# A position-bias table for eight attention heads: replicated in DRAM and read skewed, or stored once and turned round by a matrix product

## The chip, the cores and the metric

The kernel runs on one core of one Trainium2 chip. The metric is the device time of one execution in microseconds (us), taken as the median over runs. TensorE does the matrix products (PE in the profile, with its weight loads as PEld), VectorE (DVE) and ScalarE (ACT) do elementwise work, GpSimd (POOL) does some elementwise work and issues some DMAs, and SyncE (SP) issues nearly all DMAs. One DMA is carried out by up to 16 DMA engines.

## The reference, cut to what matters

The program is one decoder layer over 256 tokens with 16 meta tokens in front (L = 272 positions): layer norm, a token mixer of two parallel branches, a second norm, and a mixture of 32 experts. The part that the change touches is the relative-position bias of the sparse attention branch. `rel_bias` has 32 buckets by 8 heads, and a bucket depends on the distance between query and key alone:

```python
bias = rel_bias[t5_bucket(q_pos[None, :, None] - sel)].astype(jnp.float32)
logits = logits + jnp.moveaxis(bias, -1, 2)
```

For one head the bias of query p and key c is thus a function of c - p: a 128-row table of which each row is the row above it shifted by one place. The kernel keeps these tables as one tile `Wb` of 128 partitions x 8 heads x 272 numbers, and one tile serves both blocks of 128 queries (the first block uses its last 144 columns).

## The kernel before, in words

**The whole.** All loads of weights go through SP, in 1 MB pieces, into three rotating buffers (`load_w`, line 111; pool `wp`, `bufs=3`). ScalarE makes the high part of each weight half-piece (line 121) and VectorE the low part (line 122), and TensorE multiplies both with the normalised input. `fgroup` (line 239) is one such projection of 256 columns: two pieces, each in two halves, and after each half a call of `step()`. `step` (line 230) advances the first two generators of the list `bg`, so that small background work is laid between the halves of the large products; `drain` runs all of them to their end. The order of projections is: qk0 to qk3, mv0 to mv3, iq0 and iq1, then for each pair of heads aq, ak, av, then mo, the merge gates, the output projection, and last the experts, whose weights (some 400 MB) stream in through the same SP queue.

**The bias table.** `t5_bias` (line 301) is put on `bg` after the first projection qk0. A matrix product of `relb` and the one-hot matrix `hot` gives one row of 400 numbers for each of 8 heads, VectorE copies it to `rsb` (8 partitions x 400, line 307), and GpSimd issues a DMA (line 309) that writes every head's row 128 times into the DRAM tile `rdr` (8 x 128 x 400 numbers, 1600 KB). `t5_load` (line 311) is called after iq0: four DMAs on SP (line 314) read `rdr` back, two heads each. Their access pattern starts at element 127 and goes 399 elements from one partition to the next, so that partition p gets its head's row from element 127 - p on:

```python
late(nc.gpsimd.dma_start(out=rdr, in_=rsb.unsqueeze(1).to_broadcast([8, P, 400])))
...
in_=bass.AP(rv.tensor, rv.offset + h * P * 400 + 127, [[399, P], [P * 400, 2], [1, L]])
```

The wrapper `late` keeps an instruction in the order of the program; other instructions may be moved by the framework's scheduler.

**Who uses it.** `attend` (line 561) adds `Wb[:, h]` and a mask on GpSimd (line 564), once for each of 8 heads and 2 query blocks. Its units are put on `bg` after the first av projection. Before them, `index_scores` (line 515) is on `bg`: it scores the keys in 16 small products (`pi`, line 527), two to a step, each followed by a ScalarE activation (line 530), and picks the top keys on VectorE. These products take their PSUM tiles from the pool `px`, which has three buffers (`pxt`, line 102).

Of the kernel before, what the change touches and what calls it, by code (L numbers as in the profile page):

```python
# [11 lines left out]
F32 = mybir.dt.float32  # L12
# [5 lines left out]
ALU = mybir.AluOpType  # L18
# [4 lines left out]
P = 128  # L23
# [4 lines left out]
L = S + NM  # L28
# [3 lines left out]
AH = 8  # L32
# [15 lines left out]
def trunk(ctx, tc, x, meta, ln_emb_g, ln_emb_b, rel_bias, w_in, conv_w, conv_b, b_ig, b_fg,  # L48
          mh_g, w_pm, w_pa, w_out, ln1_g, ln1_b, w_group, b_group, w_router, b_router,
          w_gu, w_dn, ln2_g, ln2_b, t5hot, out, dbg=None):  # L50
    nc = tc.nc
    x = x[0]
    out = out[0]
# [9 lines left out]
    dram = ctx.enter_context(tc.tile_pool(name="dram", bufs=1, space=DRAM))  # L63

    late = tc.keep_in_program_order
# [36 lines left out]
    def pxt(name):  # L102
        return px.tile([P, 512], F32, name=name, tag="x")

    def pzt(name):
        return pz.tile([P, 512], F32, name=name, tag="z")
# [37 lines left out]
    ap_ = at_ctx.enter_context(tc.tile_pool(name="ap", bufs=1, side="right"))  # L144
# [7 lines left out]
    for i in (1, 2):  # L152
        for c in range(4):
# [7 lines left out]
                           in_=conv_w[0].rearrange("t (c p) -> (t c) p", p=P)))  # L161
# [11 lines left out]
    Wb = ap_.tile([P, AH, L], F32, name="Wb")  # L173
# [54 lines left out]
    bg = []  # L228
# [6 lines left out]
    def drain():  # L235
        while bg:
            step(len(bg))

    def fgroup(c0, name, t0=0, raw0=None):

        n = L - t0
        nk = 8
        pts = [pmt(f"{name}_p{i}") for i in range(2)]
        for kc in range(KD // nk):
            raw = raw0 if raw0 and not kc else load_w(w_in, kc * nk, nk, c0, 256,
                                                      f"{name}_r{kc}")
            if raw0 and kc:
                small_loads()
            for hf in range(2):
                if raw0:  # L250
                    k = kc * nk + hf * 4
                    for k in range(k + 2 if k else 0, min(k + 6, KD)):
                        embed(k)
                wh, wl = split_w(raw[:, hf * 4:hf * 4 + 4], f"{name}_{kc}{hf}")
                k0 = kc * nk + hf * 4
                for kk in range(4):
                    k = k0 + kk
                    for i in range(2):
                        for r in (xhk, xlk):
                            nc.tensor.matmul(pts[i][:, :n], lhsT=wh[:, kk, i * P:i * P + P],  # L260
                                             rhs=r(k, slice(t0, L)), start=k == 0 and r is xhk,
                                             stop=False)
                for kk in range(4):
                    k = k0 + kk
                    for i in range(2):
                        nc.tensor.matmul(pts[i][:, :n], lhsT=wl[:, kk, i * P:i * P + P],
                                         rhs=xhk(k, slice(t0, L)), start=False, stop=k == KD - 1)
                step()
        return pts
# [26 lines left out]
        late(nc.vector.tensor_copy(col[:, 0:40], pcol[:, 0:40]))  # L296
        late(nc.vector.tensor_copy(col[:, 72:136], pcol[:, 40:104]))

    rdr = dram.tile([8, P, 400], F32, name="rdr")

    def t5_bias():


        pr = pzt("pr")
        nc.tensor.matmul(pr[:8, :400], lhsT=relb, rhs=hot, start=True, stop=True)
        rsb = mp_.tile([8, 400], F32, name="rsb")
        nc.vector.tensor_copy(rsb, pr[:8, :400])
        yield
        late(nc.gpsimd.dma_start(out=rdr, in_=rsb.unsqueeze(1).to_broadcast([8, P, 400])))

    def t5_load():
        rv = rdr[:]
        for h in range(0, AH, 2):
            late(nc.sync.dma_start(
                out=Wb[:, h:h + 2],
                in_=bass.AP(rv.tensor, rv.offset + h * P * 400 + 127,
                            [[399, P], [P * 400, 2], [1, L]])))


    qk = mp_.tile([P, 8, L], F32, name="qk")  # L320
# [194 lines left out]
    def index_scores():  # L515
        pw = pzt("pw")
        for b in range(2):
            nc.tensor.transpose(pw[:, b * 16:b * 16 + 12], iwf[64:76, b * P:b * P + P],
                                ident[64:76, 64:76])
        nc.vector.tensor_copy(iw, pw[:, :32].rearrange("p (a b) -> p a b", a=2)[:, :, 4:12])  # L520
        for b in range(2):
            nk = 144 + b * 128
            s = bp.tile([P, L], F32, name=f"sc{b}", tag="sc", bufs=2)
            for h in range(8):
                r0 = (h % 2) * 64
                pi = pxt(f"pi{b}{h}")
                nc.tensor.matmul(pi[:, :nk], lhsT=iq[r0:r0 + 64, h // 2, b * P:b * P + P],
                                 rhs=ik[r0:r0 + 64, :nk], start=True, stop=True)
                rl = bp.tile([P, L], F32, name=f"rl{b}{h}", tag="rl", bufs=2)
                nc.scalar.activation(rl[:, :nk], pi[:, :nk], AF.Relu)  # L530
                if h == 0:
                    nc.vector.tensor_scalar(s[:, :nk], rl[:, :nk], iw[:, b, h:h + 1], None,
                                            op0=ALU.mult)
                else:
                    nc.vector.scalar_tensor_tensor(s[:, :nk], rl[:, :nk], iw[:, b, h:h + 1],
                                                   s[:, :nk], op0=ALU.mult, op1=ALU.add)
                if h % 2:
                    yield
            nc.gpsimd.memset(s[:, 0:NM], BIG)
            nc.gpsimd.affine_select(s[:, :nk], s[:, :nk], pattern=[[-1, nk]],  # L540
                                    compare_op=ALU.is_ge, fill=-BIG, base=16 + b * 128,
                                    channel_multiplier=1)
            w = bp.tile([P, L], F32, name=f"wk{b}", tag="wk", bufs=2)
            m8 = bp.tile([P, 8], F32, name=f"m8{b}", tag="m8", bufs=2)
            cur = s
            for r in range(TOPK // 8):
                nc.vector.max(m8, cur[:, :nk])
                nc.vector.match_replace(w[:, :nk], m8, cur[:, :nk], LOW)
                cur = w
            nc.vector.max(m8, w[:, :nk])  # L550
            nc.vector.memset(m8[:, TOPK % 8:], LOW)
            nc.vector.match_replace(w[:, :nk], m8, w[:, :nk], LOW)
            mk = msk[b]
            nc.vector.tensor_scalar(w[:, :nk], w[:, :nk], -2e38, -BIG, op0=ALU.is_gt,
                                    op1=ALU.mult)
            nc.vector.tensor_scalar(mk[:, :nk], s[:, :nk], -0.5 * BIG, -BIG, op0=ALU.is_le,
                                    op1=ALU.mult)
            nc.vector.tensor_tensor(mk[:, :nk], mk[:, :nk], w[:, :nk], op=ALU.min)
# [41 lines left out]
    def tokens_then(fts, name, v, units):  # L600
        to_tokens(fts, name, False, v)
        yield
        for g in units:
            bg.append(g)

    bg.append(index_scores())
    for j in range(AH // 2):
        pq = fgroup(O_AQ + j * 256, f"aq{j}", t0=16)
        aq = bp.tile([P, 2, S], F32, name=f"aq{j}", tag="aq", bufs=2)
        for i in range(2):  # L610
            nc.scalar.mul(aq[:, i], pq[i][:, :S], SC)
        pk = fgroup(O_AK + j * 256, f"ak{j}")
        ak = bp.tile([P, 2, L], F32, name=f"ak{j}", tag="ak", bufs=2)
        for i in range(2):
            nc.scalar.copy(ak[:, i], pk[i][:, :L])
        pv = fgroup(O_AV + j * 256, f"av{j}")
        drain()
        v = []
        units = [attend(2 * j + i, b, aq[:, i], ak[:, i], v, i * P)
                 for i in range(2) for b in range(2)]  # L620
        bg.append(tokens_then(copy_out(pv, f"av{j}"), f"av{j}", v, units))
# [574 lines left out]
    for pr_ in range(NE // 2):  # L1196
# [39 lines left out]
        if pr_ < LAST:  # L1236
            pys = [pyp.tile([P, 512], F32, name=f"py{pr_}_{c}", tag="py") for c in range(4)]
            for kk in range(4):
                ws = [next_w(), next_w()]
                for c in range(4):  # L1240
                    for i in range(2):
                        nc.tensor.matmul(pys[c][i * 64:i * 64 + 64], lhsT=hTs[i][:, kk],  # L1242
                                         rhs=ws[i][:, 0, c * 512:c * 512 + 512], start=kk == 0,
                                         stop=kk == 3)
                issue()
            pend += [lambda c=c, py=py, f=gated: f(c * 512, 512, py) for c, py in enumerate(pys)]
        else:
            flush()
            for c0, n in LASTP:
                ws = [next_w(), next_w()]  # L1250
                py = pyp.tile([P, 512], F32, name=f"py{pr_}_{c0}", tag="py")
                for kk in range(4):
                    for i in range(2):
                        nc.tensor.matmul(py[i * 64:i * 64 + 64, :n], lhsT=hTs[i][:, kk],
                                         rhs=ws[i][:, kk], start=kk == 0, stop=kk == 3)
# [17 lines left out]
    with tc.If(nmax > C):  # L1273
        with tc.For_i(0, NE, 1) as e:
# [4 lines left out]
            for part in range(2):  # L1279
                base = C + part * P  # L1280
# [13 lines left out]
                for k in range(KD):  # L1294
                    pd = op.tile([P, 512], F32, name=f"opd{k}" + nn, tag="o1")
                    for i, part in enumerate((uh, ul)):
                        for b in range(2):
                            nc.tensor.matmul(pd[:, :P], lhsT=part[:, b, rows_of(k)],
                                             rhs=oh[:, b], start=i == 0 and b == 0,
                                             stop=i == 1 and b == 1)  # L1300
# [3 lines left out]
                for kc in range(8):  # L1304
# [3 lines left out]
                    for kk in range(2):  # L1308
                        k = kc * 2 + kk
                        for i in range(2):  # L1310
                            nc.tensor.matmul(pgs[i], lhsT=xo[:, k],
                                             rhs=w[:, kk, i * 512:i * 512 + 512],
                                             start=k == 0, stop=k == KD - 1)
# [6 lines left out]
                for c in range(4):  # L1320
# [4 lines left out]
                    for kk in range(4):  # L1325
                        nc.tensor.matmul(py, lhsT=hT[:, kk], rhs=w[:, kk], start=kk == 0,
                                         stop=kk == 3)
                    nc.scalar.copy(ysb, py)
                    for b in range(2):
                        pc = op.tile([P, 512], F32, name=f"opc{c}{b}" + nn, tag="og1")  # L1330
                        nc.tensor.matmul(pc, lhsT=cwo[:, b * P:b * P + P], rhs=ysb, start=True,
                                         stop=True)
# [70 lines left out]
```

## Time and profile before

| | us |
|---|---|
| median of 3 runs | 1806.74 |
| lowest and highest of them | 1804.3, 1811.79 |
| the profiled execution | 1807.82 |
| its span, first to last instruction | 1806.1 |
| TensorE busy in the span | 1718.2 |
| VectorE, ScalarE, GpSimd busy | 711.8, 455.6, 111.0 |

The span is what the rows below are counted in: a time in a row is a distance from its start. The 1.7 us between span and execution time lie outside it. A busy share says how long an engine had an instruction in flight, not that it ran at its peak.

### The profile page before, as it was taken

What the parts mean: (1) busy time and instruction counts of PE and PEld (TensorE: products, weight loads), DVE (VectorE), ACT (ScalarE), POOL (GpSimd) and SP (SyncE); (2) the same over time, 40 slices, a digit from 0 to 9 for tenths busy, and PEclk for the clock granted to TensorE, in tenths of its full rate; (3) what the DMA queues carried; (4) which work ended last, traced back from release to release, by engine and by line L of the source; (5) the groups of instructions that cost most, each with busy time, mean ns of one, the idle gap of its engine ahead of it and who ended that gap; (6) DMA issues with size and microseconds to landing.
All of it is one profiled execution on the core that took longest, in us unless ns stands there. A gap on an engine that the chain in (4) does not pass through costs nothing. (4 is left out here: it accounts for less than half of the span.)

```text
span 1806.1 us, 21173 instructions
## 1 busy us (share of the span) xinstructions
PE 1718.2 (95%) x8626; PEld 1043.8 (58%) x8626; DVE 711.8 (39%) x1204; ACT 455.6 (25%) x703; POOL 111.0 (6%) x131
## 2 busy tenths in 40 slices
PE   8599999999999999999999999999999999999996
PEld 7598899988787877874343343333433434334332
DVE  7356774454556456552232242122112221222024
ACT  5243444444343444342010110110101101101010
POOL 3000210001122022000000000000000000000002
PEclk8799999999999999999999999999999999999998
DMA  7634454447565568458999999999999999999992
GB/s 219 129 117 142 141 164 140 148 156 247 173 213 173 198 217 295 171 212 343 419 403 408 413 356 421 421 391 421 421 420 420 422 420 421 420 422 420 421 402 71
DMA packets 155925, 538.67 MB, mean 298 GB/s; under 512 B 15772, under 2 KB 64116, under 8 KB 107680
## 3 DMA queue, kind: packets, MB, share of 16 engines
q1 hardware_dynamic: 153120, 530.54, 76.4%
q0 software_dynamic: 2640, 6.72, 1.9%
q8 instruction: 69, 1.13, 0.3%
q14 instruction: 32, 0.26, 0.0%
q10 hardware_dynamic: 64, 0.02, 0.0%
HBM read 533.50 MB, written 3.74 MB: 297 GB/s over the span
## 5 line engine op out<-in xcount | busy, mean ns | idle before, releaser
L1078 PE MATMUL gu<-we,xe 128*64 128x512 f32 x1016 | 455.9, 597 | 0.0
L1080 PE MATMUL gu<-we,xe 128*64 128x512 f32 x1016 | 454.5, 597 | 0.0
L1242 PE MATMUL py<-we,hT 128*64 128x512 f32 x960 | 276.8, 611 | 0.0
L1078 PEld LDWEIGHTS gu<-we,xe 128*64 128x64 f32 x1016 | 131.7, 137 | 244.2 <-issue 230.1
L1085 DVE TENSOR_TENSOR hb<-gu,hb 64x512 f32<-64x512 f32 x32 | 22.0, 689 | 349.1 <-ACT hb L1084 349.1
L1242 PEld LDWEIGHTS py<-we,hT 128*64 128x64 f32 x960 | 82.1, 137 | 123.8 <-issue 113.5
L1080 PEld LDWEIGHTS gu<-we,xe 128*64 128x64 f32 x1016 | 131.5, 137 | 17.2 <-issue 16.1
L1084 ACT ACTIVATE hb<-gu 64x512 f32<-64x512 f32 x32 | 18.9, 591 | 422.5 <-PE gu L1080 422.5
L1192 DVE TENSOR_TENSOR acc<-pc,acc 128x512 f32<-128x512 f32 (+1 forms) x122 | 77.5, 677 | 76.3 <-PE pc L1186 76.3
L1231 ACT ACTIVATE yh<-py,gsl 128x512 fp32r<-128x512 f32 (+1 forms) x65 | 42.7, 679 | 255.4 <-PE py L1242 178.7
L1232 DVE SCALAR_TENSOR_TENSOR yl<-py,gsl,yh 128x512 fp32r<-128x512 f32 (+1 forms) x65 | 46.7, 736 | 139.1 <-ACT yh L1231 138.7
L1009 DVE TENSOR_SCALAR xe<-pxe,gbp 128x256 f32<-128x256 f32 x64 | 34.8, 544 | 111.3 <-PE pxe L1002 111.3
L1002 PEld LDWEIGHTS pxe<-oh,uh 128*128 128x128 f32 x256 | 40.6, 197 | 48.3 <-DVE xe L1009 27.9
L1186 PE MATMUL pc<-yh,ohT 128*128 128x512 f32 (+1 forms) x130 | 53.9, 438 | 14.5 <-DVE acc L1192 11.6
L1006 ACT ACTIVATE xe<-pxe,gbp 128x256 f32<-128x256 f32 x64 | 36.0, 563 | 106.9 <-PE pxe L1002 106.9
L1002 PE MATMUL pxe<-oh,uh 128*128 128x256 f32 x256 | 59.6, 315 | 2.0 <-DMA acc<-in_w_gate_up_dram 2.0
L1178 POOL TENSOR_TENSOR fin<-acc,fin 128x512 f32<-128x512 f32 (+1 forms) x10 | 10.3, 1052 | 785.7 <-DVE acc L1192 785.7
L1186 PEld LDWEIGHTS pc<-yh,ohT 128*128 128x128 f32 x130 | 23.0, 188 | 55.6 <-issue 37.5
L1002 PE MATMUL pxe<-oh,ul 128*128 128x256 f32 x256 | 52.1, 285 | 0.0
L1186 PE MATMUL pc<-yl,ohT 128*128 128x512 f32 (+1 forms) x130 | 51.3, 418 | 0.8 <-DVE yl L1232 0.7
L1088 PEld LDWEIGHTS ph<-ident,hb 64*128 64x128 f32 x128 | 17.8, 210 | 44.3 <-DVE hb L1085 43.5
L1002 PEld LDWEIGHTS pxe<-oh,ul 128*128 128x128 f32 x256 | 41.1, 199 | 0.0
(920 smaller groups left out, 3109.7 us busy)
## 6 DMA issues: line engine op xcount, KB each, us to landing
we<-in_w_gate_up_dram SPq DMA_DIRECT2D x254, 1024.0 KB, 15.0
we<-in_w_down_dram SPq DMA_DIRECT2D x126, 1024.0 KB, 13.2
gm_r<-in_w_in_dram SPq DMA_DIRECT2D x16, 1024.0 KB, 5.0
ga_r<-in_w_in_dram SPq DMA_DIRECT2D x16, 1024.0 KB, 5.1
wo_r<-in_w_out_dram SPq DMA_DIRECT2D x16, 1024.0 KB, 5.1
qk_r<-in_w_in_dram SPq DMA_DIRECT2D x8, 1024.0 KB, 6.4
mv_r<-in_w_in_dram SPq DMA_DIRECT2D x8, 1024.0 KB, 5.3
aq_r<-in_w_in_dram SPq DMA_DIRECT2D x8, 1024.0 KB, 5.2
```

The costliest lines, as they stand in the source:

```text
L1002: nc.tensor.matmul(pt[:, :4 * C], lhsT=part[:, b, rows_of(k)], rhs=ohf[:, b], start=i == 0 and b == 0, stop=i == 1 and b == 1)
L1006: nc.scalar.activation(xe[:, k], pt[:, :4 * C], AF.Identity, bias=gbp[:, 1, k:k + 1], scale=gbp[:, 0, k:k + 1])
L1009: nc.vector.tensor_scalar(xe[:, k], pt[:, :4 * C], gbp[:, 0, k:k + 1], gbp[:, 1, k:k + 1], op0=ALU.mult, op1=ALU.add)
L1078: nc.tensor.matmul(pg_[other], lhsT=lt, rhs=w[:, kk, 0:512], start=k == 0, stop=k == KD - 1)
L1080: nc.tensor.matmul(pg_[mine], lhsT=lt, rhs=w[:, kk, 512:1024], start=k == 0, stop=k == KD - 1)
L1084: nc.scalar.activation(hb[mine], pg_[other], AF.Silu)
L1085: nc.vector.tensor_tensor(hb[mine], pg_[mine], hb[mine], op=ALU.mult)
L1186: nc.tensor.matmul(pc[:, :n], lhsT=ohT[:, b * P:b * P + P], rhs=y[:, :n], start=i == 0, stop=i == 1)
L1192: nc.vector.tensor_tensor(av, pc[:, :n], av, op=ALU.add)
L1231: nc.scalar.activation(yh[:, :n], py[:, :n], AF.Copy, scale=gate)
L1232: nc.vector.scalar_tensor_tensor(yl[:, :n], py[:, :n], gate, yh[:, :n].bitcast(F32), op0=ALU.mult, op1=ALU.subtract)
L1242: nc.tensor.matmul(pys[c][i * 64:i * 64 + 64], lhsT=hTs[i][:, kk], rhs=ws[i][:, 0, c * 512:c * 512 + 512], start=kk == 0, stop=kk == 3)
```

## The change

The row of each head is written to DRAM once (8 x 400 numbers). The read-back keeps four DMAs of two heads, 128 partitions and rows of 272, but partition p starts at element p of its head's row, so that the rows of the table arrive in reverse order. A new generator `t5_flip` makes an anti-diagonal one-hot matrix `anti` with two GpSimd instructions, then for each head multiplies `anti` with `Wb[:, h]` on TensorE, which puts the rows in the right order in PSUM, and copies the result back into `Wb[:, h]` on ScalarE. It is put on `bg` behind `index_scores`, and yields after `anti` and after each head.

```diff
-    rdr = dram.tile([8, P, 400], F32, name="rdr")
+    rdr = dram.tile([8, 400], F32, name="rdr")
...
-        late(nc.gpsimd.dma_start(out=rdr, in_=rsb.unsqueeze(1).to_broadcast([8, P, 400])))
+        late(nc.gpsimd.dma_start(out=rdr, in_=rsb))
...
-                in_=bass.AP(rv.tensor, rv.offset + h * P * 400 + 127,
-                            [[399, P], [P * 400, 2], [1, L]])))
+                in_=bass.AP(rv.tensor, rv.offset + h * 400, [[1, P], [400, 2], [1, L]])))
+
+    def t5_flip():
+        anti = ap_.tile([P, P], F32, name="anti")
+        nc.gpsimd.memset(anti, 0.0)
+        nc.gpsimd.affine_select(anti, anti, pattern=[[1, P]], compare_op=ALU.not_equal, fill=1.0,
+                                base=1 - P, channel_multiplier=1)
+        yield
+        for h in range(AH):
+            pw = pxt(f"pfl{h}")
+            nc.tensor.matmul(pw[:, :L], lhsT=anti, rhs=Wb[:, h], start=True, stop=True)
+            nc.scalar.copy(Wb[:, h], pw[:, :L])
+            yield
...
     bg.append(index_scores())
+    bg.append(t5_flip())
```

## Rows read from the trace of the kernel before

**Rows 1.** Stretches: length, busy us of PE, PEld, DVE, ACT, POOL, clock, DMA, GB/s.

```profile
60.00:70.00 10.00, 3.18 (x26) 2.97 (x24) 0.00 (x0) 0.00 (x0) 0.00 (x0) 0.79 0.50 56
70.00:80.00 10.00, 0.00 (x0) 0.00 (x0) 0.00 (x0) 0.00 (x0) 0.00 (x0) 0.50 0.53 83
80.00:90.00 10.00, 7.60 (x47) 7.61 (x48) 6.87 (x11) 3.90 (x5) 0.00 (x0) 0.69 0.80 264
...
210.00:220.00 10.00, 10.00 (x83) 9.32 (x80) 6.03 (x13) 4.75 (x11) 0.42 (x2) 1.00 0.41 121
...
1300.00:1400.00 100.00, 96.13 (x415) 35.58 (x412) 21.08 (x35) 9.69 (x17) 0.00 (x0) 1.00 1.01 420
```

**Rows 2.** Waits: engine, line, releaser: us in total, times, longest.

```profile
PE qk_p L260 <- ACT qk_00h L121: 19.2, 1, 19.2
...
ACT qk_00h L121 <- DMA qk_r<-in_w_in_dram: 23.7, 1, 23.7
...
SPq L808 <- PE wo_p L284: 22.1, 5, 10.8
```

**Rows 3.** DMA issues: count, KB each, median us from issue to landing.

```profile
aq_r<-in_w_in_dram SPq DMA_DIRECT2D x8, 1024.0 KB, 5.2
...
rdr<-rsb POOLq DMA_DIRECT2D x1, 1600.0 KB, 36.6
Wb<-rdr SPq DMA_DIRECT2D x4, 272.0 KB, 5.9
...
mhg<-in_mh_norm_g_dram POOLq DMA_DIRECT2D x1, 512.0 KB, 3.7
```

**Rows 4.** Line 309's issue (ns, start us); queue in 60:82 (packets, MB, engines' share).

```profile
L309 POOL DMA_DIRECT2D rdr<-rsb x1: 1117/1117/1117, 42.7 to 42.7; - x1
...
q0 software_dynamic: 194, 0.88, 39.9%
```

**Rows 5.** SP's issues in order of time: start us, us, what.

```profile
58.55 19.59 SPq L113 DMA_DIRECT2D mv_r<-in_w_in_dram  x1
...
148.50 2.28 SPq L314 DMA_DIRECT2D Wb<-rdr  x4
166.41 5.10 SPq L113 DMA_DIRECT2D iq_r<-in_w_in_dram  x2
```

**Rows 6.** PE in order of time around the gap: start us, us, [idle before].

```profile
62.02 1.17 PE L266 MATMUL qk_p<-xh,qk_11l 128*128 128x272 f32 x8
...
82.40 0.60 PE L260 MATMUL qk_p<-xh,qk_00h 128*128 128x272 f32 x1 [19.21 <-ACT qk_00h L121]
...
86.19 1.18 PE L266 MATMUL qk_p<-xh,qk_00l 128*128 128x272 f32 x8
87.20 0.29 PE L260 MATMUL qk_p<-xh,qk_01h 128*128 128x272 f32 x1
```

**Rows 7.** PE in order of time, later: plain f32 products, and a short gap.

```profile
187.20 0.70 PE L461 MATMUL pn<-mv3b,e 128*128 128x257 f32 x2
187.83 0.70 PE L461 MATMUL pn<-mv3m,e 16*128 16x257 f32 x2
...
202.05 1.22 PE L266 MATMUL iq_p<-xh,iq_11l 128*128 128x256 f32 x8 [1.14 <-DVE iq_11l L122]
...
253.72 0.86 PE L566 MATMUL pl<-ak,aq 128*128 128x144 f32 x4
254.22 0.48 PE L260 MATMUL aq_p<-xh,aq_11h 128*128 128x256 f32 x1
```

**Rows 8.** ACT and POOL in order of time; line 402 (min/median/max ns).

```profile
182.98 1.05 ACT L121 CAST iq_00h<-iq_r 128x1024 fp32r<-128x1024 f32 x1 [0.41 <-ACT e L443]
...
219.32 1.05 ACT L121 CAST ak_10h<-ak_r 128x1024 fp32r<-128x1024 f32 x1 [1.45 <-PE ak_p L260]
...
L402 ACT COPY av0f<-av_p x2: 380/385/390, 244.8 to 245.0; 128x272 f32<-128x272 f32 x2
...
218.99 0.11 POOL L539 MEMSET sc<- 128x16 f32 x1 [16.41 <-issue]
```

## The prediction, made before the change was run

> **What bounds the kernel now.** I read the busy stretches first. TensorE is full nearly everywhere: 10.0 of 10 us in a stretch of the attention projections, 96.1 of 100 in a stretch of the expert stage, where the DMA engines also read 1.01 of their time and move 420 GB/s [rows 1]. So there are two regimes: up to the experts the pace is that of TensorE, behind it that of the weight stream. The reader should see one hole in the first regime: between 60 and 80 us TensorE works 3.2 us of 20, VectorE, ScalarE and GpSimd nothing at all, the granted clock falls to 0.50, and yet the DMA engines are busy for about half of their time while they move only 56 and 83 GB/s [rows 1].
>
> The list of waits names it: TensorE waited once for 19.2 us for the cast of a qk piece, and ScalarE, which makes that cast, waited 23.7 us for the DMA that brings the piece [rows 2]. A 1 MB piece of the same form lands in 5.2 us elsewhere [rows 3]. What lay on the engines at that time is the write of the bias table: one DMA of 1600 KB, issued by GpSimd at 42.7, which took 36.6 us to land, thus to 79.3 (or a little later, counted from the end of its 1.1 us issue) [rows 3, 4]. In 60 to 82 us its queue holds 39.9% of the sixteen engines' time [rows 4], as eight fully taken engines until 79 would. SP's issue of the next piece hangs for 19.59 us from 58.55 on, to 78.1, where the write ends [rows 5]; and in the next ten us the rate is 264 GB/s [rows 1]. The write moves 44 KB per us and the weight pieces are spread over the same engines, so each piece ends with its slowest part.
>
> **Part 1, the write: removed work.** It shrinks from 1600 KB to 8 rows of 1600 bytes, 12.8 KB. What the hole costs is read from TensorE's order [rows 6]. The last eight products before it begin at 62.02, and eight such take 1.01 us (86.19 to 87.20), so the next would begin at 63.03. It begins at 82.40, 19.4 us late. [...] Bounds: 19.2 (the wait alone) and 21.1; I take 21.1, because both parts have the same cause.
>
> All compute engines stood still in the hole, so no other work was hidden in it that would now have to be done elsewhere. What is late next? Once the hole is gone a 1 MB piece must come every 2 x 3.03 us (a half-piece is 16 products of 2.02 us and 8 of 1.01), and it lands in 5.2 us with three buffers to run ahead; the same supply keeps TensorE at 10.0 of 10 in the stretch at 210 [rows 1, 3]. I therefore put nothing against the 21.1.
>
> [...]
>
> **Part 2, the new write and the read-back: same issues, other addresses.** GpSimd still issues one DMA and SP four, with the same 1088-byte rows into the same partitions. The new write is read more than 80 us later [rows 4, 5], so even the old write's 36.6 us would be covered: 0 us. The read-back takes from 148.50 to 150.78 to issue and 5.9 us to land, so 1088 KB in 8.2 us, to 156.7 [rows 3, 5]. Nothing waits for it before the flips some 50 us later. Its new form reads the same two 1600-byte rows for all partitions. The nearest row is the load of `mhg`, which spreads one 4 KB row over 128 partitions: 512 KB in 3.7 us, 138 GB/s [rows 3], which would make 7.9 us here. Bounds: no change, or a slow read (third rival); I take 0, by the `mhg` row.
>
> **Part 3, the flips: added work on TensorE.** Eight products of plain f32, 128x128 by 272 columns, stand among the projections aq0, ak0 and av0, where TensorE is full [rows 1], so they lengthen the path. Price: a plain f32 product of 257 columns (two MATMUL entries) takes 0.63 us from its start to the next (187.20 to 187.83), 0.67 for 272 columns; two of 144 columns take 0.50 (253.72 to 254.22), 0.47 each for 272 [rows 7]. Eight cost 3.8 to 5.3 us. If the scheduler moves some into gaps such as the 1.14 us before 202.05 [rows 7], 2.7 is left; there is nothing by which they could gain. I take the 257-column row as it is the nearest, 0.63 x 8 = 5.0 us.
>
> **Part 4, what goes beside them.** Eight ScalarE copies of 128x272 from PSUM cost 0.385 us each, 3.1 us in all; each has the 1.45 us that ScalarE idles before the next cast, which itself waits for TensorE [rows 8]. Cost 0; 3.1 us if that cover were gone. GpSimd's two instructions for `anti` come while it idles for 16.41 us before 218.99 [rows 8]: cost 0; without that cover the first flip and the products behind it would wait for them, about half a us. New waits: the flip waits for the read-back (landed long before), its copy for the flip, and behind the copy stands ScalarE's next cast; the units of the attention wait for the copies, but they come only after av0 and a `drain`. 0 us.
>
> **Sum.** The profiled execution took 1807.82 us, a span of 1806.1 and 1.7 around it. 1807.8 - 21.1 + 5.0 = 1791.7, a span of 1790.0. It reaches the end undiminished, since the expert stream begins when TensorE frees its buffers (SP waits there for the output projection's products [rows 2]), so the stream moves forward as a whole. The median of the runs, 1806.74, is 1.1 below the profiled execution; on that footing the forecast is 1790.6, and I say 1791.
>
> **Rivals.**
>
> 1. The flips hold TensorE. The score products take two of the three PSUM buffers of their pool at each step, the flip the third. If a flip's copy came to stand behind a ScalarE cast (1.05 us [rows 8]), the next step's first product could wait for cast and copy, 1.05 + 0.39 = 1.44 us, eight times 11.5 us. Then 1791.7 + 11.5 = 1803.2, 1802 on the median's footing. For it: the buffers are just used up. Against it: a step lasts over 3 us, and the copy has 1.45 us of idle ScalarE.
>
> 2. The hole is not the write's, so that the change doesn't remove it: the piece came late for another reason, the 19.2 us stay, and the flips come on top: 1807.8 + 5.0 = 1812.8, 1812 on the median's footing. For it: the write and the piece run on different queues, and 44 KB per us is little. Against it: the piece's lateness and SP's hanging issue end at the very time at which the write lands, and 39.9% of the engines' time is the write's queue [rows 4, 5].
>
> 3. The slower side: the read-back of one row by all partitions is slow. It takes 8.2 us now. The next load is issued at 166.41, lands 5.2 us later, and its cast at 182.98 waited for other work [rows 3, 5, 8]; so the read-back may last until 177.8, that is 29.3 us, before the cast is late. From there each us is TensorE's, and the gain of 16.1 is gone at 45.4 us, or 24 GB/s. At an eighth of the `mhg` rate, 17.3 GB/s, it takes 62.9 us: a new hole of 33.6, 1791.7 + 33.6 = 1825.3, 1824 on the median's footing. Against it: `mhg` itself, 138 GB/s out of a single row [rows 3]. [...]
>
> **How the numbers follow.** Forecast 0.83, rival 1 0.07, rival 2 0.05, rival 3 0.03, something better than forecast (flips in gaps and shorter loads) 0.02. The forecast's own range: gain 19.2 to 21.1, flips 2.7 to 5.3, and a spread of medians of a few us (the three runs of before reach from 1804.3 to 1811.8) make 1787 to 1797. The range given is 1786 to 1800, which takes in part of rival 1. A measurement can tell about 0.5% from no change, 9 us: faster means below 1797.7. The forecast and what is better are faster (0.85), and of rival 1 a share of 0.02 where the holding is short, 0.87; rival 2 and the rest of rival 1 are no change, 0.10; rival 3 is slower, 0.03.
>
> **What would show it.** Right: the write lands within 10 us; the stretch of 60 to 80 us shows TensorE full and the clock at 1.00; no single TensorE wait of over 5 us is left before the experts; sixteen new MATMUL entries appear, and the projections from aq0 to av0 last about 5 us longer; the expert stream starts some 16 us earlier and lasts as long. Wrong: a TensorE wait for a qk or iq piece that remains or appears, or flips that are followed by idle time on TensorE.

## The result, and the profile after

| | before | after |
|---|---|---|
| median of 6 runs each (us) | 1808.61 | 1793.39 |
| lowest and highest | 1804.30, 1812.47 | 1785.70, 1794.38 |
| profiled execution | 1807.82 | 1794.38 |
| its span | 1806.1 | 1792.7 |
| mean granted clock in the span | 0.981 | 0.986 |

The ratio of the times is 0.9906 (95% interval 0.9881 to 0.993): faster by 15.2 us in the medians and by 13.4 us between the two profiled executions. The forecast was 1791 in a range of 1786 to 1800, and 16.1 us of gain.

The busy stretches of the kernel after, in the columns of [rows 1]:

```profile
60.00:70.00 10.00, 10.00 (x82) 10.00 (x81) 6.96 (x11) 4.28 (x5) 0.00 (x0) 1.00 0.64 201
70.00:80.00 10.00, 10.00 (x81) 10.00 (x81) 6.24 (x10) 3.88 (x5) 0.00 (x0) 1.00 0.44 132
80.00:90.00 10.00, 10.00 (x82) 10.00 (x81) 5.19 (x11) 3.61 (x8) 0.00 (x0) 1.00 0.60 195
```

The hole is gone. Where TensorE had worked 3.2 us of 20 [rows 1], it now works all 20, at a granted clock of 1.00. The list of waits, in the columns of [rows 2], has no wait of TensorE above 3.1 us ahead of the experts (`pn` stands at the very end of the kernel); one that was 0.8 us before, `pws`, is now 2.3:

```profile
PE gm_p L284 <- DVE gm_01l L122: 5.6, 3, 3.1
PE pn L1370 <- DVE nm L1366: 4.5, 1, 4.5
PE pws L722 <- DVE wsum L719: 2.3, 1, 2.3
```

The DMA issues of the kernel after, as in [rows 3], and its new instructions tile by tile (duration in ns as least, median, greatest; first and last start in us):

```profile
rdr<-rsb POOLq DMA_DIRECT2D x1, 12.5 KB, 3.1
Wb<-rdr SPq DMA_DIRECT2D x4, 272.0 KB, 5.9
```

```profile
L326 PE MATMUL pfl<-Wb,anti x16: 390/393/497, 189.4 to 218.3; 128*128 128x272 f32 x16
L327 ACT COPY Wb<-pfl x8: 386/388/390, 190.1 to 218.7; 128x272 f32<-128x272 f32 x8
```

The write lands in 3.1 us where it took 36.6 [rows 3], and the read of one row by 128 partitions lands in the same 5.9 us as the skewed read of 128 copies. Sixteen MATMUL entries and eight copies are new.

To see where the time went I followed landmarks through ScalarE's, VectorE's and TensorE's order of time (start, duration, what): the activation behind projection iq1, the copy behind av0, the last sum of the merge gates' statistics, the first expert's input, and a product at the end. The kernel before, then the kernel after:

```profile
203.18 0.66 ACT L501 ACTIVATE iq<-iq_p 128x256 f32<-128x256 f32 x2
244.77 0.67 ACT L402 COPY av0f<-av_p 128x272 f32<-128x272 f32 x2
570.25 1.37 DVE L707 TENSOR_REDUCE wsum<-wgr 128x40 f32<-128x640 f32 x1
815.45 0.56 ACT L1006 ACTIVATE xe<-pxe,gbp 128x256 f32<-128x256 f32 x1
1793.42 0.66 PE L1358 MATMUL pn<-ident,nm 128*128 128x128 f32 x2 [4.48 <-DVE nm L1354]
```

```profile
182.43 0.66 ACT L512 ACTIVATE iq<-iq_p 128x256 f32<-128x256 f32 x2
227.72 0.67 ACT L413 COPY av0f<-av_p 128x272 f32<-128x272 f32 x2
553.29 1.38 DVE L719 TENSOR_REDUCE wsum<-wgr 128x40 f32<-128x640 f32 x1
800.30 0.56 ACT L1018 ACTIVATE xe<-pxe,gbp 128x256 f32<-128x256 f32 x1
1779.95 0.66 PE L1370 MATMUL pn<-ident,nm 128*128 128x128 f32 x2 [4.49 <-DVE nm L1366]
```

The lead of the kernel after is 20.75 us at iq1, 17.05 at av0, 16.96 at the merge gates, 15.15 at the first expert and 13.47 at the end. So the hole gave 20.75 us (21.1 forecast), the flips cost 3.70 (5.0 forecast), and 3.58 that were not in the forecast got lost later: 0.09 up to the merge gates, 1.81 between these and the experts, 1.68 in the expert stage.

The 1.81 us can be followed. TensorE's order of time of the kernel before, then of the kernel after, around the merge gates (in brackets the idle time ahead and who ended it):

```profile
567.24 1.89 PE L284 MATMUL gm_p<-gm_01l,xh 128*128 128x512 f32 x4 [3.06 <-DVE gm_01l L122]
568.93 1.06 PE L755 MATMUL pmt<-ident,gms 128*128 128x128 f32 x4
...
571.68 0.45 PE L710 MATMUL pws<-wsum,ones 128*128 128x80 f32 x2 [0.84 <-DVE wsum L707]
```

```profile
550.28 1.20 PE L284 MATMUL gm_p<-gm_01l,xh 128*128 128x512 f32 x4 [3.08 <-DVE gm_01l L122]
551.32 0.60 PE L767 MATMUL pmt<-ident,gms 128*128 128x128 f32 x4
...
554.72 0.45 PE L722 MATMUL pws<-wsum,ones 128*128 128x80 f32 x2 [2.33 <-DVE wsum L719]
...
557.57 1.99 PE L284 MATMUL gm_p<-gm_10l,xh 128*128 128x512 f32 x4
```

In both kernels TensorE idles some 3.1 us for `gm_01l` and later waits for `wsum`. Before, the products in between run at a lowered clock (0.58 on the mean of 567 to 570; 1.89 us for four where after shows 1.20), and they are done 0.84 us ahead of `wsum`. After, they run fast, so TensorE waits 2.33 us for the same `wsum`, and the slow products come behind the wait (1.99 us for four). Stretches of the kernel before, then after:

```profile
567.00:570.00 3.00, 2.76 (x9) 2.25 (x10) 3.00 (x3) 1.42 (x2) 3.00 (x2) 0.58 0.54 138
```

```profile
553.00:556.00 3.00, 1.28 (x6) 1.08 (x7) 3.00 (x7) 0.00 (x0) 1.33 (x3) 0.99 0.77 277
556.00:559.00 3.00, 3.00 (x10) 2.40 (x9) 2.66 (x4) 1.42 (x3) 0.00 (x0) 0.50 0.48 108
```

A fall of the clock whose cost the wait for `wsum` had partly covered has moved to where nothing covers it: 0.50 on the mean of 556 to 559, while TensorE is full. What made it fall later in one kernel than in the other no run here shows. The flips are neither enough for it nor needed: from that last sum for `wsum` to the first expert's input it takes 245.20 us before and 247.01 after, 245.30 with the flips alone and 246.85 in a kernel without any (both below, the second with every fourth source partition).

In the expert stage the stretch of [rows 1] and its neighbour read, after:

```profile
1200.00:1300.00 100.00, 96.69 (x419) 38.62 (x415) 23.16 (x43) 12.70 (x22) 0.00 (x0) 0.98 1.01 421
1300.00:1400.00 100.00, 96.95 (x430) 38.15 (x431) 17.77 (x32) 10.04 (x19) 0.00 (x0) 0.98 1.01 421
```

The DMA engines are as busy as before and move as much; the granted clock is 0.98 where it was 1.00 [rows 1]. Such a 0.98 is one short fall of the clock. Closer up, in the kernel after:

```profile
1200.00:1208.00 8.00, 8.00 (x36) 2.43 (x32) 0.06 (x1) 0.59 (x1) 0.00 (x0) 1.00 1.02 421
1208.00:1216.00 8.00, 7.45 (x29) 2.98 (x29) 2.91 (x11) 0.37 (x1) 0.00 (x0) 0.79 1.01 420
1216.00:1224.00 8.00, 8.00 (x40) 3.25 (x38) 0.00 (x0) 0.00 (x0) 0.00 (x0) 1.00 1.01 418
```

A clock of 0.79 on the mean of 8 us is a loss of 1.7 us at full speed; TensorE was busy all of the 8 us ahead of it, and the weight stream runs on unchanged. From 900 us on, the kernel after has four such falls (0.98 in the four stretches from 1200 to 1600), the kernel before three (0.98 from 900 to 1000 and from 1500 to 1600, 0.97 from 1700 to 1750). The 1.68 us are this one fall. The twelve traces of this case, those of the experiments below among them, agree: from the first expert's input to the product at the end four of them take 974.3 to 974.7 us, two 978.0 to 978.1, two 979.6 to 979.7 and four 981.2, and behind the start of the stage these groups have none or one, three, four and five falls. Why there are more of them in one execution than in another no run here shows.

### The profile page after: what moved, and what is told of

The parts are those of the page before. It is cut to its first block, busy times and chain, and to the rows that moved or that the text cites. A ratio compares the mean times of both kernels' runs of the same rounds, so it can differ in the third digit from the quotient of the medians.

```text
span 1792.7 us, 21232 instructions
## 1 busy us (share of the span) xinstructions
PE 1723.0 (96%) x8642; PEld 1046.9 (58%) x8642; DVE 713.6 (40%) x1204; ACT 459.3 (26%) x711; POOL 111.8 (6%) x133
## 5 line engine op out<-in xcount | busy, mean ns | idle before, releaser
L1014 PEld LDWEIGHTS pxe<-oh,uh 128*128 128x128 f32 x256 | 40.5, 197 | 48.3 <-DVE xe L1021 28.7
L1198 PE MATMUL pc<-yh,ohT 128*128 128x512 f32 (+1 forms) x130 | 54.0, 438 | 14.5 <-DVE acc L1204 11.6
```

The lines of the kernel that those rows point to most:

```text
L1014: nc.tensor.matmul(pt[:, :4 * C], lhsT=part[:, b, rows_of(k)], rhs=ohf[:, b], start=i == 0 and b == 0, stop=i == 1 and b == 1)
L1198: nc.tensor.matmul(pc[:, :n], lhsT=ohT[:, b * P:b * P + P], rhs=y[:, :n], start=i == 0, stop=i == 1)
```

## The experiments

My theory: the hole came from the 1600 KB write, so one row per head removes it, and the flips cost their own time and no more. The rivals: flips that hold TensorE, a hole with another cause, and (raised by the result) a cost of the flips that some other version need not pay. Each run's time is set beside a run of the kernel before on the same chip. Up to the last group each time is a single execution, and single executions of one kernel differ by more than the flips cost, so the argument rests on waits, landings and landmarks and not on these times.

### The flips alone

Kernel before, with eight products of the identity, and copies, at the place of the flips; the large write stays.

```diff
+            nc.tensor.matmul(pw[:, :L], lhsT=ident, rhs=Wb[:, h], start=True, stop=True)
+            nc.scalar.copy(Wb[:, h], pw[:, :L])
...
     bg.append(index_scores())
+    bg.append(t5_flip())
```

> The kernel before with eight products and copies added at the place of the flips, but with the identity in place of the anti-diagonal matrix; the 128-fold write and the skewed read stay. Theory (the write makes the hole, the flips only lengthen the path): the TensorE wait of 19.2 us stays, the 1600 KB write still lands in 36.6 us, and from the end of iq1 to the end of av0 the projections last 3.7 us longer than before (as in the changed kernel), span about 1806.1 + 3.7 = 1809.8. Rival (the price of the prediction holds and something else gave 1.3 us back in the changed kernel): 5.0 us longer, span 1811. Rival (the products at that place disturb or help something early): the hole changes.

1809.43 us against 1807.07. Its list of waits, and ScalarE's order of time at the two landmarks around the flips:

```profile
PE qk_p L260 <- ACT qk_00h L121: 20.2, 1, 20.2
```

```profile
204.34 0.66 ACT L509 ACTIVATE iq<-iq_p 128x256 f32<-128x256 f32 x2
249.62 0.66 ACT L410 COPY av0f<-av_p 128x272 f32<-128x272 f32 x2
```

The stretch from iq1 to av0 takes 45.28 us, 3.69 more than before (41.59); in the kernel after it was 45.29. So the flips cost 3.7 us, 0.46 each, with the hole in front of them as without it. The hole stays (the write lands in 37.6 us here).

### Half the bytes

The large write with 64 copies of each row in place of 128, read back in eight DMAs of 64 partitions; no flips.

```diff
+    rdr = dram.tile([8, 64, 400], F32, name="rdr")
...
+        late(nc.gpsimd.dma_start(out=rdr, in_=rsb.unsqueeze(1).to_broadcast([8, 64, 400])))
```

> The kernel before with 64 instead of 128 copies of each row (800 KB), read back by eight DMAs of 64 partitions; no flips. Theory (the write holds eight DMA engines for a time that goes by its bytes, and the weight piece lands when it ends): the write lands in about 18.3 us, at 61 us, the late piece at about 63, its cast ends at 64, and the TensorE wait of 19.2 us shrinks to about 1 us; TensorE keeps its clock there; span about 1786. Rival (the hole belongs to the place in the program and not to the write): wait of 19.2 us and span of 1806 as before.

1794.68 us against 1807.07. The write takes 18.9 us, half of 36.6, and the wait shrinks with it (list of waits):

```profile
PE qk_p L260 <- ACT qk_00h L121: 2.4, 1, 2.4
ACT qk_00h L121 <- DMA qk_r<-in_w_in_dram: 6.9, 1, 6.9
```

The hole follows the length of the write. The span, 1793.0 us, is 7.0 above what I had expected; its lead at av0 is 18.83 us (225.94 against 244.77), and of that 5.89 us are lost by the end (1780.48 against 1793.42 for the last product): 2.51 between the merge gates and the experts, where the clock is 0.50 on the mean of 548 to 558, and 3.27 in the expert stage, with five falls of the clock against three.

### Sixteen engines

The product makes every row 16 times, on 128 partitions, and each partition writes 8 copies: the same 1600 KB, now with 128 as the outermost size of the DMA.

```diff
+        nc.tensor.matmul(pr[:, :400], lhsT=relb16.rearrange("p a b -> p (a b)"), rhs=hot,
+                         start=True, stop=True)
...
+        late(nc.gpsimd.dma_start(
+            out=rdr.rearrange("h (c j) x -> (h c) j x", c=16),
+            in_=rsb.unsqueeze(1).to_broadcast([P, 8, 400])))
```

> The kernel before with the same 1600 KB written to the same places, but from 128 partitions (16 per head, made by the same product with repeated columns), each of which writes its row 8 times; no flips. Theory (the write is long because its source has 8 partitions, which keeps it to 8 of the 16 engines): the write lands in about half, 18 us, the TensorE wait shrinks to about 1 us, span about 1786. Rival (its bytes, the DRAM side or the software queue set its length): it still takes about 36 us, the wait stays near 19 us or is shared by more engines, span about 1806.

1788.71 us against 1807.07. The DMA issues:

```profile
rdr<-rsb POOLq DMA_DIRECT2D x1, 1600.0 KB, 7.6
```

I had expected 18 us, half of the old time, from twice the engines. It is a fifth, and there is no hole at all, with all the bytes of the kernel before. The queue of the write in its first 8 us (44:52; packets, MB, share of the 16 engines):

```profile
q0 software_dynamic: 368, 1.64, 54.6%
```

54.6% of 16 engines for 8 us is 70 us of engine time for the whole write. In the kernel before, the same 1.64 MB (44:79):

```profile
q0 software_dynamic: 704, 1.64, 46.9%
```

That is 263 us of engine time. So each byte holds an engine far longer when it comes from partitions 0 to 7: it isn't only that fewer engines work.

### Another queue

The large write issued by ScalarE in place of GpSimd.

```diff
-        late(nc.gpsimd.dma_start(out=rdr, in_=rsb.unsqueeze(1).to_broadcast([8, P, 400])))
+        late(nc.scalar.dma_start(out=rdr, in_=rsb.unsqueeze(1).to_broadcast([8, P, 400])))
```

> The kernel before with its 128-fold write issued by ScalarE instead of GpSimd, all else as it was. Theory (eight engines, whatever the queue): the write still takes 30 to 40 us, the TensorE wait stays between 13 and 23 us, span 1800 to 1810. Rival (GpSimd's queue makes it slow): it lands in under 15 us, the wait is gone, span about 1786.

1802.88 us against 1807.07; its profile has no landing time for this DMA, but from 42 to 82 us its queue holds 36.2% of the sixteen engines, where that of the kernel before holds 41.0%. The list of waits:

```profile
PE qk_p L260 <- ACT qk_00h L121: 17.6, 1, 17.6
```

The hole is 1.6 us shorter and stays in kind, so the issuing engine is not the cause.

### The write one projection later

`t5_bias` put on `bg` after qk1 in place of qk0; all else as before.

```diff
         if j == 0:
...
+            small_loads2()
+        if j == 1:
             bg.append(t5_bias())
-            small_loads2()
```

> The kernel before with the generator of the table put on the background list one projection later (after qk1 instead of qk0), so that the same 1600 KB write begins some 12 us later, at about 55 us. Theory (a weight piece issued into the write lands when the write ends): nothing happens at 63 us, the wait of 17 to 22 us appears one projection (12 us) later, at 69 to 76 us, for a piece of qk3 or mv0, and the span stays at 1803 to 1809. Rival (the hole belongs to what qk3 does at 63 us): a wait at 63 us as before.

1813.60 us against 1811.34. The write is issued at 53.9 and takes 36.6 us again. Its stretches (as [rows 1]) and waits:

```profile
60.00:70.00 10.00, 10.00 (x82) 10.00 (x81) 7.59 (x12) 3.92 (x5) 0.00 (x0) 1.00 0.77 144
70.00:80.00 10.00, 4.38 (x35) 4.17 (x34) 0.00 (x0) 0.00 (x0) 0.00 (x0) 0.93 0.51 59
80.00:90.00 10.00, 0.00 (x0) 0.00 (x0) 0.00 (x0) 0.00 (x0) 0.00 (x0) 0.50 0.49 68
```

```profile
PE mv_p L260 <- ACT mv_00h L121: 19.3, 1, 19.3
```

The hole moves 11 us with the write, hits another piece (`mv` in place of `qk`) and keeps its size, 19.3 against 19.2 us [rows 2]. This settles that the write makes the hole.

### Eight source partitions, spread

Two kernels that keep eight source rows, eight as the outermost size and all 1600 KB, and change only which partitions of `rsb` hold the rows: every fourth (0, 4, ... 28), or every sixteenth (0, 16, ... 112).

```diff
+        nc.vector.tensor_copy(wide, relb.unsqueeze(2).to_broadcast([32, 8, 4]))
...
+        late(nc.gpsimd.dma_start(out=rdr, in_=rsb[::4].unsqueeze(1).to_broadcast([8, P, 400])))
```

> The kernel before with the same 128-fold write of 1600 KB from 8 partitions, but from partitions 0, 4, 8 to 28 instead of 0 to 7; no flips. [...] Engines theory (8 source partitions mean 8 DMA engines, and each is slow by itself): 30 to 38 us, wait near 19 us, span about 1806.

> As the run with partitions 0, 4 to 28, but with the source on partitions 0, 16, 32 to 112; no flips. [...] Plain distance (the farther apart the better): no longer than with a step of 4. Engines theory: 30 to 38 us, wait near 19 us.

Every fourth: 1789.06 us against 1811.34, the write lands in 12.0 us, no hole. Every sixteenth: 1790.70, 21.6 us, and a small hole. The DMA issues of the first, of the second, and the wait in the second:

```profile
rdr<-rsb POOLq DMA_DIRECT2D x1, 1600.0 KB, 12.0
```

```profile
rdr<-rsb POOLq DMA_DIRECT2D x1, 1600.0 KB, 21.6
```

```profile
PE qk_p L260 <- ACT qk_00h L121: 4.8, 1, 4.8
```

With eight source partitions and eight as the outermost size, the same bytes take 36.6, 21.6 or 12.0 us by where the eight lie; from all 128 partitions, with 128 as the outermost size, they take 7.6. So what mostly sets the length is which partitions are read. How much of the engines is taken does not tell the three kernels with eight source partitions apart: the write's queue, while the write runs, holds 48.0% of the sixteen engines in the kernel before (50 to 70 us), 48.3% with every sixteenth partition (46 to 62), 49.6% with every fourth (46 to 53), in each about what eight fully taken engines would show. With all 128 partitions it holds 96.9% (46 to 50). Twice the share by itself would have made the sixteen-engine write 18 us (an estimate: 36.6 us times 48.0 over 96.9).

Two things go together. The first is how many engines are taken, about eight in three of the kernels and sixteen in the fourth by these shares; whether that goes by the outermost size or by the number of source partitions no run here shows, as the two were changed together. The second is how long each is held, and that goes by where the source lies: the whole write takes 263, 132, 74 and 70 us of engine time (46.9% from 44 to 79; 20.6% and 11.6% from 42 to 82; 54.6% from 44 to 52). Why neighbouring partitions hold the engines longer no run here shows either. Between every fourth partition and all 128 the engine time is nearly the same; the step from 12.0 to 7.6 us goes with the number of engines.

### No flips: the row mirrored, and the large write spread, timed

The first kernel writes one row per head like the kernel after, but with the row itself reversed: the one-hot table is built backward, and the user of `Wb` reads its columns backward in place of a product that turns the rows.

```diff
+                in_=bass.AP(rv.tensor, rv.offset + h * 400 + 1, [[1, P], [400, 2], [1, L]])))
...
+        nc.gpsimd.tensor_tensor(wm[:, :nk], Wb[:, h, nk - 1::-1], msk[b][:, :nk], op=ALU.add)
...
+    rel = np.maximum(np.arange(400) - 128, 0)
```

The second is the sixteen-engine write once more, and the third the kernel after once more.

> A single row per head is written, as in the changed kernel, but the one-hot table holds its columns in reverse order, the read-back goes one element forward per partition, and the attention reads the table backwards along its row; no flips. Theory (the gain is the 1600 KB write alone, the flips cost 3.7 us): no hole, no lengthening between iq1 and av0, about 3.7 us faster than the changed kernel, 1788 to 1791, ratio to the kernel before about 0.989. Rival (reading backwards slows GpSimd's sixteen additions and through them the attention): av0 to av3 last longer, 1792 or more.

> The kernel with the whole 1600 KB written from 128 partitions, timed: no hole and no flips, so the same as the mirrored version, 1787 to 1791, ratio to the kernel before about 0.989; faster than the changed kernel by 3 to 5 us.

> The changed kernel itself beside them on the same chip: 1791 to 1795, ratio to the kernel before 0.988 to 0.993; its three stretches as in its first profile (20.8 us earlier at the end of iq1, 17.1 at av0), while the granted clock's short falls and the expert stage may come out differently by 1 to 4 us.

| | median (us) | lowest, highest | ratio to before, 95% interval |
|---|---|---|---|
| before (11 runs) | 1811.03 | 1804.41, 1813.68 | |
| row mirrored (5 runs) | 1784.11 | 1780.69, 1792.19 | 0.9854, 0.9832 to 0.9876 |
| sixteen engines (6 runs) | 1784.22 | 1780.60, 1793.53 | 0.9870, 0.9841 to 0.9898 |
| kernel after (6 runs) | 1793.58 | 1785.50, 1796.30 | 0.9894, 0.9870 to 0.9918 |

ScalarE's order of time of the mirrored kernel:

```profile
181.77 0.66 ACT L500 ACTIVATE iq<-iq_p 128x256 f32<-128x256 f32 x2
223.37 0.66 ACT L401 COPY av0f<-av_p 128x272 f32<-128x272 f32 x2
```

From iq1 to av0 it takes 41.60 us, as before (41.59): without flips the 3.7 us are saved. The backward read costs nothing that shows: from av0 to av3, beside the attention units, it takes 126.85 us against 126.86 before. Both versions beat the kernel after by about 9.4 us in the median, more than the 3.7 that the flips cost. In the lowest runs the distance is 4.8 and 4.9. An execution of one kernel varies by over 10 us along with the mean granted clock of its span (mirrored: 1780.69 at 0.990, 1792.19 at 0.983; after: 1785.50 at 0.989, 1796.30 at 0.983), and the interval of the kernel after overlaps those of the other two ratios. The profiled sixteen-engine execution, at 1783.49, shows a clock of 1.00 in both of the expert stretches in which the kernel after had 0.98. That flips bring such falls about is not borne out by the traces: with the flips alone the expert stage takes 974.57 us, in the mirrored kernel without flips 981.16, in the kernel after 979.65 and, once more, 979.62 (the landmarks of its two profiles agree within 0.04 us). Whether they have a part in how often an execution is a long one, some 5 us in the medians, stays open.

## Why the prediction was right

- **What bounded the kernel: right.** The write caused the hole. Moved, halved or spread over partitions, it moved, shrank or removed the hole (19.3 us at another piece; 2.4; none).
- **Part 1, 21.1 us: right, 20.75 measured.** Counting the half-clock products with the wait was needed: the wait alone was 19.2, the lower bound. The 21.1 is 19.4 us by which the next product began late and 1.8 by which the sixteen products behind the wait ran long, 3.79 us at a granted clock of 0.50 (82.0 to 86.2) where two times eight take 2.02 [rows 6]. The 1.8 is worked out from the kernel before, and no run shows it by itself; the lead at iq1, 20.75, shows the two together. My reason for the slow write, eight engines fully taken, was half of it: about as many were taken in the spread writes too (48.3 and 49.6% of sixteen), for a half and for little more than a quarter of the engine time (132 and 74 us against 263). The other half is which partitions the source lies on.
- **Part 2, 0 us: right.** 5.9 us to land, as before. The `mhg` row was the right neighbour; reading one row at places four bytes apart is not slow here.
- **Part 3, 5.0 us: mis-sized, 3.70 measured.** I took 0.63 us from the start of one product pair to the next, 187.20 to 187.83 [rows 7], as that of a steady run (and left it at 257 columns; 0.67 for 272 would have made 5.3). But the five products of that group, from 186.58 to 189.24, take 2.66 us, 0.53 each, and some of them have 16 rows in place of 128; why three of the starts lie 0.62 to 0.63 apart was not tested. The other bound, the 144-column products at 0.47 us for 272 columns [rows 7], was right (0.46). Number of columns was the wrong sense of nearest; a row among full projections would have been nearer.
- **Part 4, 0 us: right.** Copies of 0.388 us; TensorE does not wait for them, and the flips alone cost the same 3.7 us on top of the kernel before. The scheduler also put the two instructions for `anti` near the start of the kernel, at 1.0 and 1.5 us.
- **The sum: 16.1 us forecast, 15.2 in the medians, 13.4 between the profiled executions.** With its terms as measured it is 20.75 less 3.70, 17.05, and that is the lead at av0. The step that failed is "it reaches the end undiminished": 3.58 us got lost behind av0, 1.81 around the merge gates, where a fall of the clock came behind the wait for `wsum` and no longer ahead of it (the wait is 2.33 against 0.84), and 1.68 by one more fall in the expert stage. The reason given for that step, that behind the first expert the weight stream sets the pace and moves forward as a whole, is not what the traces show. TensorE's list has no wait for a weight piece behind the first expert's input, in either kernel, and its weight loads wait for one at most 0.4 us at a time, while the queue that issues the pieces waits for TensorE's products to free buffers (592 us in all between 830 and 1760 in the kernel before, against 175 for earlier transfers); so what TensorE loses there comes out at the end. The forecast came near in part by luck: 0.35 us too much gain and 1.30 too much cost offset 0.95 of the 3.58, and the medians gained 1.8 us more than the profiled executions.
- **The rivals.** Flips that hold TensorE: refuted by the 3.7 us of the flips alone. Another cause of the hole: refuted by the write moved and the write spread. A slow read-back: refuted by the 5.9 us.

## What to carry to other kernels

A DMA out of a few neighbouring SBUF partitions can hold the DMA engines for several times as long as the same bytes from spread partitions do (263 against 70 us of engine time), and a transfer that runs beside it can then end late, as the qk piece did (ScalarE waited 23.7 us for it [rows 2]); look for a stretch with busy DMA engines, few GB/s and idle compute engines. Before shrinking such a write, try to spread its source over partitions: here that removed the whole hole with all the bytes kept, and without the 3.7 us of products that the smaller write had to pay for. And a gain in the middle reaches the end only so far as later waits and falls of the clock let it: check landmarks, not the end alone.

## What the hardware showed that was not expected

- 1600 KB from SBUF to DRAM: 36.6 us from partitions 0 to 7, 21.6 from every sixteenth, 12.0 from every fourth, 7.6 from all 128. While the first three run, their queue holds 48.0, 48.3 and 49.6% of the sixteen engines, for 263, 132 and 74 us of engine time in all.
- In steady expert work, TensorE full and the weight stream unchanged at 421 GB/s, the granted clock is 0.98 in one execution and 1.00 in another, and executions of one kernel differ by over 10 us along with it (1780.60 to 1793.53 for one of them). One fall costs 1.7 us, and the expert stages of the twelve traces differ by whole falls.
- Where a fall of the clock comes decides what it costs: at the merge gates products ran slowed ahead of a wait before (1.89 us for four), which covered most of it, and behind that wait after (1.99 us for four), where all of it showed: the wait was 0.84 us before and 2.33 after.
